# Attention scores: store tiles of 4 MB in runs of 32 KB, in place of 2 MB in runs of 16 KB

## Chip, cores, metric

One Trainium2 chip, one core. Its engines are PE (matrix products), ACT, DVE and POOL (elementwise work), and SP, which here issues the DMAs; 16 DMA engines carry the data. The metric is the device time of one execution in microseconds (us), the median of several runs. Spans in the profile are about 1.8 us shorter than that time.

## The reference

Inputs q and k of shape (8, 8, 512, 64): batch, heads, rows, dim. The output is `q @ k^T / 8` per head, (8, 8, 512, 512) in float32. 16.8 MB are read and 67.1 MB written.

```python
def reference(q, k):
    scale = 1.0 / np.sqrt(q.shape[-1])
    return (np.einsum('bhqd,bhkd->bhqk', q, k) * scale).astype(np.float32)
```

## The kernel before

The work goes in four units of two batches. Inputs are loaded, cast to bf16, transposed on PE, and copied into `kT` and into `qz`, a zero-padded block form with two heads in the 128 contraction rows. One matmul with 128 stationary columns then gives 64 rows of each of two heads. An output tile `o` holds 8 rows per partition (16 KB in one run), 2 MB in all, and four of them rotate. An eviction is the scaled copy of a finished product out of PE's accumulator memory into `o`.

```python
RO = 8                                   # output rows per partition
out_r = out.rearrange("(v b) (n h) (u i) k -> v (b n) (h u) (i k)", b=2, h=2, i=RO)
raw_pool = ...bufs=3    # xf, 16 KB per partition: one input tensor of one unit
out_pool = ...bufs=4    # o, 16 KB per partition
psum_pool = ...bufs=3   # ps, [128, 2, 512] f32, two banks
# ... cuts
def scores(v, n):
    kT, qz = ts[v]
    o = out_pool.tile([P, RO, S], f32, name="o")
    for i in range(0, RO, 2):
        ps = psum_pool.tile([P, 2, S], f32, name="ps")
        for w in range(2):
            nc.tensor.matmul(out=ps[:, w, :], lhsT=qz[:, i + w, n, :], rhs=kT[:, n]...)
        evacuate(o[:, i:i + 2, :], ps)    # x 1/8, alternately on ACT and DVE
        yield                             # steps of the next unit's transposes go in between
    nc.sync.dma_start(out=out_r[v, n], in_=src)
```

All loads and stores are issued from one queue (SP).

## Time and profile before

| | before |
|---|---|
| time, median (lowest to highest) | 204.17 us (204.15 to 204.36) |
| span in the profile, instructions in it | 202.3 us, 1549 |
| DVE, PE, ACT busy | 64%, 52%, 51% |
| loads and stores, share of 16 DMA engines' span | 97.7% |

The prediction below reads this profile. Two lines of the page's DMA section, not used there, become important later. They are the queues that fetch instructions. The columns are packets, MB, and share of the 16 engines' span.

```profile
q8 instruction: 4, 0.07, 0.1%
q14 instruction: 4, 0.03, 0.0%
```

In the trace's single DMA records, q8 carries packets of 16 KB and q14 packets of 8 KB.

### The profile page before, as it was taken

To read this page: it belongs to the slowest core of one execution; us is meant where nothing else is said; L and a number is where in the kernel's file an instruction comes from. 1 tells how busy PE (TensorE), PEld (TensorE's weight loads), DVE (VectorE), ACT (ScalarE), POOL (GpSimd) and SP (SyncE) were. 2 spreads that over 40 slices of the span, in tenths; PEclk is the share of its full clock that TensorE was granted. 3 is DMA by queue.
4 is the path that set the end of the run, shared out by engine and by line. 5 is a ranking of instruction groups with operands and counts; after the bars stand their busy time and mean duration, and the time that the engine had idled before them with its cause. 6 is when DMAs were issued, how large, how long until landed. Compare 5 with 4: busy or idle time off the path is not lost.

```text
span 202.3 us, 1549 instructions
## 1 busy us (share of the span) xinstructions
PE 106.1 (52%) x512; PEld 50.2 (25%) x512; DVE 129.6 (64%) x133; ACT 102.5 (51%) x130; POOL 26.8 (13%) x20
## 2 busy tenths in 40 slices
PE   0045557755854755858575575656564677642000
PEld 0034424432211322423222233223121222210000
DVE  6875669987765686878787788777544455553000
ACT  2254457967654448484756666574833344442000
POOL 1037775756000000000000000000000000000000
PEclk9999999978799699797979787896969655695555
DMA  6999999999999999999999999999999999999991
GB/s 214 428 441 428 424 441 421 424 395 434 437 421 434 432 423 431 434 428 428 437 424 431 431 424 434 434 428 431 434 428 428 431 434 428 428 437 429 416 447 75
DMA packets 5768, 83.99 MB, mean 415 GB/s; under 512 B 640, under 2 KB 640, under 8 KB 640
## 3 DMA queue, kind: packets, MB, share of 16 engines
q1 hardware_dynamic: 5760, 83.89, 97.7%
q8 instruction: 4, 0.07, 0.1%
q14 instruction: 4, 0.03, 0.0%
HBM read 16.78 MB, written 67.11 MB: 415 GB/s over the span
## 4 chain that ended last, share of the span: by engine, by line
DMA 52%; ACT 13%; DVE 13%; PE 10%; issue 2%; ACTq 0%; DVEq 0%; SPq 0%
DMA out_dram<-o 52%; ACT o L62 6%; DVE o L64 5%; PE ps L134 5%; ACT qz L99 4%; DVE qz L89 3%; ACT kT L99 3%; PE tp L120 3%; DVE kT L99 3%; PE tp L111 2%; DVE xb L83 1%; DVE qz L99 1%; ACTq L62 0%; DVEq L64 0%; SPq L140 0%
## 5 line engine op out<-in xcount | busy, mean ns | idle before, releaser
L134 PE MATMUL ps<-kT,qz 128*128 128x512 bf16 x256 | 87.3, 470 | 52.4 <-ACT o L62 43.3
L64 DVE TENSOR_SCALAR o<-ps 128x1024 f32<-128x1024 f32 x64 | 78.2, 1225 | 44.1 <-DMA out_dram<-o 28.5
L62 ACT ACTIVATE o<-ps 128x1024 f32<-128x1024 f32 x64 | 63.5, 1022 | 64.3 <-DMA out_dram<-o 50.9
L134 PEld LDWEIGHTS <-qz 128*128 128x128 bf16 x256 | 28.6, 115 | 98.6 <-issue 87.2
L83 POOL CAST xb<-xf 128x2048 bf16<-128x2048 f32 x14 | 26.1, 1893 | 21.5 <-DMA xf<-in_q_dram 18.1
L99 DVE COPY kT<-tp 64x512 bf16<-64x512 bf16 x32 | 22.0, 687 | 4.3 <-PE tp L111 3.8
L99 DVE COPY qz<-tp 64x512 bf16<-64x512 bf16 x32 | 22.0, 687 | 4.2 <-PE tp L120 3.7
L111 PE MATMUL tp<-identity,xb 128*128 128x128 bf16 x128 | 13.0, 267 | 17.0 <-DVE xb L83 11.1
L99 ACT COPY kT<-tp 64x512 bf16<-64x512 bf16 x32 | 18.5, 578 | 5.0 <-PE tp L111 4.7
L99 ACT COPY qz<-tp 64x512 bf16<-64x512 bf16 x32 | 18.5, 577 | 4.2 <-PE tp L120 3.9
L120 PE MATMUL tp<-identity,xb 128*128 128x128 bf16 x128 | 13.3, 271 | 8.1 <-ACT qz L99 4.9
L111 PEld LDWEIGHTS <-xb 128*128 128x128 bf16 x128 | 11.2, 122 | 21.3 <-ACT xb L83 11.1
L120 PEld LDWEIGHTS <-xb 128*128 128x128 bf16 x128 | 11.5, 123 | 12.6 <-issue 9.7
L89 DVE MEMSET qz<- 64x2048 uint32 x4 | 7.1, 1765 | 2.6 <-issue 1.4
L83 ACT CAST xb<-xf 128x2048 bf16<-128x2048 f32 x1 | 1.9, 1898 | 6.7 <-DMA xf<-in_k_dram 6.7
L83 ACT ACT_TABLE_LOAD x1 | 1.3, 1283 | 0.7 <-PEq L181 0.7
L83 DVE CAST xb<-xf 128x2048 bf16<-128x2048 f32 x1 | 1.2, 1227 | 0.0
masks.py:199 POOL TENSOR_SCALAR_AFFINE_SELECT identity<-identity 128x128 bf16<-128x128 bf16 x1 | 0.3, 292 | 0.1
masks.py:197 POOL MEMSET identity<- 128x128 bf16 x1 | 0.2, 205 | 0.3 <-POOLq L181 0.3
L181 POOL MEMSET const-float32-0.0<- 128x1 f32 x1 | 0.1, 98 | 0.2 <-issue 0.2
L181 POOL MEMSET const-bfloat16-1.0<- 128x1 bf16 x1 | 0.1, 101 | 0.0
L181 POOL MEMSET const-uint8-127<- 128x1 uint8 x1 | 0.1, 101 | 0.0
(1 smaller groups left out, 0.1 us busy)
## 6 DMA issues: line engine op xcount, KB each, us to landing
out_dram<-o SPq DMA_DIRECT2D x32, 2048.0 KB, 16.1
xf<-in_k_dram SPq DMA_DIRECT2D x4, 2048.0 KB, 11.3
xf<-in_q_dram SPq DMA_DIRECT2D x4, 2048.0 KB, 12.3
```

The source lines that it names most:

```text
L62: pinned(nc.scalar.mul(out=dst, in_=src, mul=scale))
L64: pinned(nc.vector.tensor_scalar(out=dst, in0=src, scalar1=scale, scalar2=None, op0=mybir.AluOpType.mult))
L83: pinned(copy(out=xb[:, :, s, :], in_=xf[:, s].rearrange("p (j d) -> p j d", j=J)))
L89: nc.vector.memset(qz[half(h), :, :, (1 - h) * U:(2 - h) * U], 0.0)
L99: pinned(copy(out=dst(s, h), in_=src[:, h]))
L111: pinned(nc.tensor.transpose(out=tp[:, j, :], identity=identity, in_=kb[:, j0 + j].rearrange("p s d -> p (s d)")))
L120: pinned(nc.tensor.transpose(out=tp[:, i, jj, :], identity=identity, in_=qb[:, RO * jj + i0 + i].rearrange("p s d -> p (s d)")))
L134: pinned(nc.tensor.matmul(out=ps[:, w, :], lhsT=qz[:, i + w, n, :], rhs=kT[:, n].rearrange("d m s j -> d (m s j)"), start=True, stop=True))
L181: nc = _bacc.Bacc("TRN2", target_bir_lowering=False, num_devices=1)
```

## The change

The intent: longer runs per store, so fewer DMA packets and fewer stores. A partition now holds 16 rows (32 KB in one run). A head then fills only 32 partitions, so a tile takes four heads: two head pairs, each in a 64-column tile of PE, side by side. 4 MB tiles need 32 KB per partition. Three such buffers are shared by inputs and outputs.

```diff
-    RO = 8
+    RO = 16
+    TILES = N // 2
-    out_r = out.rearrange("(v b) (n h) (u i) k -> v (b n) (h u) (i k)", b=2, h=2, i=RO)
+    out_r = out.rearrange("(v b) (t h) (u i) k -> v (b t) (h u) (i k)", b=2, h=4, i=RO)
-    raw_pool (bufs=3), out_pool (bufs=4), bf_pool (bufs=5)
+    big_pool (bufs=3), bf_pool (bufs=6)
-        if n_evac % 2 == 0:
+        if n_evac % 6 in (0, 2, 3):
 # load_and_cast: one buffer for k and q of a unit; all casts on GpSimd
-                if v == 0 and src is k_r:
-                    copy = (nc.vector.tensor_copy, nc.scalar.copy)[s]
 # scores
+        o = big_pool.tile([P, RO, S], f32, name="big")
             for w in range(2):
-                matmul(out=ps[:, w, :], lhsT=qz[:, i + w, n, :], rhs=kT[:, n]...)
+                for x in range(2):
+                    matmul(out=ps[half(x), w, :], lhsT=qz[:, i, 2 * t + x, :], rhs=kT[:, 2 * t + x]...)
-        nc.sync.dma_start(out=out_r[v, n], in_=src)
+        nc.sync.dma_start(out=out_r[v, t], in_=src)
```

(In the last matmul line `i` stands for `i + w`.) PE gets 512 matmuls and weight loads of 64 columns in place of 256 of 128, which is 512 more PE instructions.

More of the change, by code (lines that the diff above doesn't have):

```diff
@@ L42 @@
     k_r = k.rearrange("(v b) g (m j) d -> v (b g m) (j d)", b=2, j=R)
-    out_r = out.rearrange("(v b) (n h) (u i) k -> v (b n) (h u) (i k)", b=2, h=2, i=RO)
+    out_r = out.rearrange("(v b) (t h) (u i) k -> v (b t) (h u) (i k)", b=2, h=4, i=RO)
     consts = ctx.enter_context(tc.tile_pool(name="consts", bufs=1))
-    raw_pool = ctx.enter_context(tc.tile_pool(name="raw", bufs=3))
-    bf_pool = ctx.enter_context(tc.tile_pool(name="bf", bufs=5))
+    big_pool = ctx.enter_context(tc.tile_pool(name="big", bufs=3))
+    bf_pool = ctx.enter_context(tc.tile_pool(name="bf", bufs=6))
     t_pool = ctx.enter_context(tc.tile_pool(name="t", bufs=2))
-    out_pool = ctx.enter_context(tc.tile_pool(name="out", bufs=4))
     tpsum_pool = ctx.enter_context(tc.tile_pool(name="tpsum", bufs=2, space=bass.MemoryType.PSUM))
@@ L71, in load_and_cast @@
     def load_and_cast(v):
+        xf = big_pool.tile([P, 2, 2, J * D], f32, name="big")
         both = []
-        for src in (k_r, q_r):
-            xf = raw_pool.tile([P, 2, J * D], f32, name="xf")
-            nc.sync.dma_start(out=xf, in_=src[v])
+        for x, src in enumerate((k_r, q_r)):
+            nc.sync.dma_start(out=xf[:, x], in_=src[v].rearrange("p (s c) -> p s c", s=2))
+        for x in range(2):
             xb = bf_pool.tile([P, J, 2, D], bf16, name="xb")
             for s in range(2):
-                if v == 0 and src is k_r:
-                    copy = (nc.vector.tensor_copy, nc.scalar.copy)[s]
-                else:
-                    copy = nc.gpsimd.tensor_copy
-                pinned(copy(out=xb[:, :, s, :], in_=xf[:, s].rearrange("p (j d) -> p j d", j=J)))
+                pinned(nc.gpsimd.tensor_copy(out=xb[:, :, s, :],
+                                             in_=xf[:, x, s].rearrange("p (j d) -> p j d", j=J)))
             both.append(xb)
         return both
-    def clear(qz, h):
-        nc.vector.memset(qz[half(h), :, :, (1 - h) * U:(2 - h) * U], 0.0)
     def rearrange(tp, pattern, dst):
@@ L125, in transpose, with matmul, scores @@
                                  .rearrange("d i n (m s jj) -> d s i n m jj", s=2, jj=JJ)[:, s])
-    def scores(v, n):
+    def matmul(v, t, i, x, dst):
         kT, qz = ts[v]
-        o = out_pool.tile([P, RO, S], f32, name="o")
+        pinned(nc.tensor.matmul(out=dst, lhsT=qz[:, i, 2 * t + x, :],
+                                rhs=kT[:, 2 * t + x].rearrange("d m s j -> d (m s j)"),
+                                start=True, stop=True))
+    def scores(v, t):
+        o = big_pool.tile([P, RO, S], f32, name="big")
         for i in range(0, RO, 2):
@@ L133, in scores @@
             for w in range(2):
-                pinned(nc.tensor.matmul(out=ps[:, w, :], lhsT=qz[:, i + w, n, :],
-                                        rhs=kT[:, n].rearrange("d m s j -> d (m s j)"),
-                                        start=True, stop=True))
+                for x in range(2):
+                    matmul(v, t, i + w, x, ps[half(x), w, :])
             evacuate(o[:, i:i + 2, :], ps)
@@ L147 @@
     make_identity(nc, identity)
-    qzs = [consts.tile([P, RO, N, P], bf16, name=f"qz{n}") for n in range(2)]
+    qzs = [consts.tile([P, RO, N, 2 * U], bf16, name=f"qz{n}") for n in range(2)]
     for qz in qzs:
-        for h in range(2):
-            clear(qz, h)
+        nc.vector.memset(qz, 0.0)
     cast = [load_and_cast(v) for v in range(UNITS)]
@@ L158 @@
         ahead = transpose(v + 1, *cast[v + 1]) if v + 1 < UNITS else iter(())
-        per_step = 3 if v == 0 else 1
-        for n in range(N):
-            take(ahead, 1)
-            for _ in scores(v, n):
-                take(ahead, per_step)
+        for t in range(TILES):
+            for n, _ in enumerate(scores(v, t)):
+                take(ahead, 1 + (n % 4 == 3) if v else 2 * (t > 0))
         for _ in ahead:
```

## The prediction

> **What bounds the kernel now.** I read the page's busy shares and its DMA lines first, because 84 MB have to cross the DMA engines whatever the cores of the kernel do.
>
> ```profile
> span 202.3 us, 1549 instructions
> PE 106.1 (52%) x512; PEld 50.2 (25%) x512; DVE 129.6 (64%) x133; ACT 102.5 (51%) x130; POOL 26.8 (13%) x20
> ...
> DMA  6999999999999999999999999999999999999991
> ...
> q1 hardware_dynamic: 5760, 83.89, 97.7%
> ```
>
> No compute engine is over 64%. The DMA row is at nine tenths or more in every slice but the first and the last, and the one queue that carries all loads and stores fills 97.7% of 16 engines' span. The average could still hide a stage, so next the busy times by stretch.
>
> ```profile
> 0.00:5.00 5.00, 0.00 (x0) 0.00 (x0) 3.31 (x2) 1.28 (x1) 0.70 (x6) 1.00 0.68 216
> 5.00:30.00 25.00, 9.56 (x75) 8.01 (x76) 17.00 (x22) 11.34 (x18) 12.91 (x7) 1.00 1.00 430
> 30.00:50.00 20.00, 12.80 (x84) 7.32 (x83) 18.30 (x22) 15.92 (x23) 13.20 (x8) 0.90 1.01 421
> 50.00:100.00 50.00, 31.70 (x147) 13.84 (x146) 35.53 (x36) 28.93 (x35) 0.00 (x0) 0.87 1.01 430
> ...
> 195.00:202.30 7.30, 0.00 (x0) 0.00 (x0) 0.00 (x0) 0.00 (x0) 0.00 (x0) 0.50 0.44 189
> ```
>
> The columns after the window's length are PE, PE weight loads, DVE, ACT, POOL, then granted clock, DMA share and GB/s. DMA is full from 5 us to 195 us at 421 to 430 GB/s, also across the switch from loads to stores (30 to 50 us), the one place where compute is dense: DVE 18.3 of 20 us. Third, the waits.
>
> ```profile
> ACT o L62 <- DMA out_dram<-o: 50.9, 24, 3.0
> DVE o L64 <- DMA out_dram<-o: 28.5, 24, 2.0
> ```
>
> The evictions wait for a store to free their output buffer: compute is ahead of DMA by all four buffers. The chain of waits agrees: its largest part is the stores, 52%, in pieces of about 15 to 16 us, three or four queued stores long. So the end is set by: DMA starts at 1.7 us, each of 16 engines carries 320 packets of 16 KB plus 40 semaphore writes, and the tail. In the trace's single DMA records 4487 of the 5120 data packets took 611 ns and 635 of 640 semaphore writes 9 ns. That gives 320 x 0.611 + 40 x 0.009 = 195.9 us per engine; slow packets bring the mean to 197.6. The last data end at 201.0 us, though most engines are done by 198 to 199: a tail of some 2.5 us of unevenness.
>
> **What the Trainium skill says.** "DMA: Bandwidth & Descriptors", section "Where 436 GB/s comes from", puts the ceiling at 16 ports x 32 B x 850 MHz, 435.2 GB/s, or 27.2 GB/s per engine. 16 KB would then take 602.4 ns; the trace has 611, so at most 8.6 ns (1.4%) is not payload. The same page, section "Why small descriptors are slow (HBM only)", tells of a fixed cost of about 3 cycles per packet, 3.5 ns at that clock. The 9 ns of a 4-byte write is the size of the leftover too, which makes a fixed cost per packet plausible; no run so far separates it from a slightly lower rate per byte. On the matmuls, "TensorEngine Tiling (Array Packing)", section "Key Properties", says that tiles work in parallel, and its restrictions that column tiling turns off the fast weight load. "TensorE: Matmul & The Clock Gate", section "Measured speedup vs the span model", has 2.38x for three column tiles. The kernel before has no column tiles, so its trace can't agree or disagree.
>
> **The change part by part.**
>
> Stores. 32 stores of 2 MB become 16 of 4 MB; per engine 256 packets of 16 KB become 128 of 32 KB, if the packet follows the run. Loads keep their 64 packets of 16 KB. If the 8.6 ns are paid per packet, a 32 KB packet takes 2 x 602.4 + 8.6 = 1213.4 instead of 1222 ns: 128 x 0.0086 = 1.1 us less. Sixteen fewer DMAs save 16 x 0.009 = 0.14 us. Together 1.25 us, all on the path that sets the end, since DMA is never idle. This is all that the change can bring in the long run; even a perfect ceiling for all bytes (83.89 MB / 435.2 GB/s = 192.8 us against 197.6 busy) would be 4.8 us or 2.35%, and the loads aren't touched.
>
> Compute per 4 MB tile, off the path. It must fit under the 8 x 1.213 = 9.7 us of a store. One unit of four tiles (38.8 us) has 32 evictions: 16 on DVE and 16 on ACT, in a new pattern of three to three that changes no totals. DVE: 16 x 1.225 + 16 rearranging copies x 0.687 = 30.6 us. ACT: 16 x 1.022 + 16 x 0.578 = 25.6 us. Both fit, as now. PE: 128 matmuls of 64 columns in place of 64 of 128. From the warm stretches (four in 1.03 us, one alone 0.377) one starts each 0.218 us, so in parallel pairs 64 x 0.218 = 14 us and 5 us of transposes; strictly one after the other 28 + 5 = 33 us, still under 38.8, but with little room for waits.
>
> Buffers. Three of 4 MB in place of four of 2 MB. In the steady state a freed buffer has the two other stores, 19.4 us, less some 3 us of issue and landing, to be filled by 8 evictions and their copies, 8 to 10 us. Before it was 3 x 4.9 = 14.7 us less the same 3 for 4 to 5 us of work. Slack stays.
>
> The start, where the change could lose. Two things move. The first casts leave DVE and ACT: POOL does all, 1.87 us each and two per tensor. And the first store needs 8 evictions into a buffer that held the inputs of unit 1. The start of before, from the timeline:
>
> ```profile
> 8.68 1.90 ACT L83 CAST xb<-xf 128x2048 bf16<-128x2048 f32 x1 [6.66 <-DMA xf<-in_k_dram]
> ...
> 11.08 1.86 PE L111 MATMUL tp<-identity,xb 128*128 128x128 bf16 x16 [11.08 <-DVE xb L83]
> ...
> 13.58 3.73 POOL L83 CAST xb<-xf 128x2048 bf16<-128x2048 f32 x2 [12.28 <-DMA xf<-in_q_dram]
> ...
> 28.73 1.91 PE L134 MATMUL ps<-kT,qz 128*128 128x512 bf16 x4
> ...
> 34.34 39.41 SPq L140 DMA_DIRECT2D out_dram<-o  x9
> ```
>
> Key 0 lands at 8.7 in both; POOL is done with it at 8.7 + 3.7 = 12.4, so transposes begin 1.4 us later, and with the same 17 us of transposes and copies the first scores start near 29.3. Query 0 is cast by 13.6 + 3.7 = 17.3, before it is needed near 20.8. Inputs land every 4.9 us, so POOL keeps up: unit 1 is cast at 27 us (its buffer is free before 29.3), unit 2 at 37, unit 3 at 47. With the PE clock still low (a matmul each 0.43 us in before at 29 us) an eviction needs 0.86 us of parallel pairs: first eviction near 30.3, the eighth done near 30.3 + 7 x 0.9 + 1.2 = 37.8. The DMA queue has loads until about 1.7 + 64 x 0.611 + 0.9 (slow first packets) = 41.7. The first store is there 3 us early. The second tile, with two steps of the next transposes per eviction, takes some 9 us: 47, needed at 51. The third, in unit 3's buffer: 56, needed at 61. From there slack grows. No hole in the DMA row, then.
>
> Sum: 204.17 - 1.25 = 202.9 us.
>
> **The rivals.**
>
> *The 611 ns is a rate per byte.* Then 32 KB takes 1222 ns, and only the semaphores are saved: 204.0 us. For it: the 8.6 ns are inferred by a nominal clock. Against: the semaphore writes' 9 ns. I give it a third.
>
> *Column pairs run one after the other,* because a weight load for the other half waits, or without the fast load isn't hidden. Then an eviction costs 1.7 us at the low clock and 0.87 warm; the first tile is ready near 41 to 42 us, the DMA row gets a hole of about 1 us, and every tile with transposes takes 10 to 12 us against 9.7: 205 to 212 us. For it: alternate halves, twice the number of weight loads, PEclk falling to 5 or 6 tenths in places. Against: the skill's measured parallel column tiles;[...] compute has some 20 to 25% to spare.
>
> *Longer runs load the memory unevenly,* or engines drift apart more with packets twice as long. One step is 1.2 us in the tail, and the tail is already 2.5 us, set by one or two late engines: plus or minus 2 us, so 201 to 205. Nothing in before speaks of slower stores than loads: both take 611 ns.
>
> *A gain of over 2%* would need all bytes at the ceiling and a shorter tail as well. Nothing speaks for it.
>
> **Range and chances.** I take 203.1, between the first sum (202.9) and the rate-per-byte case (204.0), nearer the first. The range is 201.6 to 206.0: below by a shorter tail, above by a hole of 1 to 3 us at the start. Within 2% is 200.1 to 208.2. Faster 0.03, slower 0.07 (serial pairs that pace the tiles), within 0.90.
>
> **What would show it.** Store packets of 1213 ns (fixed cost) or 1222 (rate), or 16 KB packets in unchanged number (the run doesn't set the packet). The DMA row at nine all the way, above all at 40 to 45 us; first store issued before 41 us. Matmuls of the two halves starting a few ns apart, against 0.2 us or more. Evictions still waiting for stores, in sum near 80 us. The prediction is wrong if evictions wait chiefly for PE after 60 us, if a hole of over 3 us follows the loads, or if store packets take over 1240 ns.

## The result

The changed kernel takes 203.82 us (203.74 to 203.86, 4 runs) against 204.16 us before. The ratio is 0.9981, 95% interval 0.9964 to 0.9998. Ratios here are the mean time of one kernel's fast runs over that of the other's in the same rounds, so not quite the ratio of the quoted medians. The direction was right and the time lies in the range, but the gain is 0.34 us where 1.07 us were forecast.

The page of the changed kernel: span and instructions, busy time by engine, the DMA row by slice, and the DMA queues.

```profile
span 202.1 us, 1976 instructions
PE 107.7 (53%) x768; PEld 55.7 (28%) x768; DVE 126.4 (63%) x130; ACT 101.1 (50%) x129; POOL 30.5 (15%) x22
...
DMA  6999999999999999999999999999999999999991
...
q1 hardware_dynamic: 3456, 83.89, 97.2%
q8 instruction: 6, 0.10, 0.2%
q14 instruction: 2, 0.02, 0.0%
```

DMA is full as before, with no hole after the loads. The share of the data queue fell from 97.7 to 97.2% in almost the same span: there is more time in which some DMA engine is done. There are six large instruction fetches in place of four. The stretches of the changed kernel (window length; PE, PE weight loads, DVE, ACT, POOL; granted PE clock, DMA share, GB/s):

```profile
30.00:50.00 20.00, 12.12 (x108) 6.71 (x109) 14.37 (x17) 13.51 (x18) 13.10 (x8) 0.99 1.03 428
50.00:100.00 50.00, 35.06 (x278) 17.29 (x274) 42.96 (x47) 34.60 (x45) 0.00 (x0) 0.90 1.00 430
100.00:150.00 50.00, 35.11 (x227) 16.57 (x225) 35.81 (x37) 29.87 (x38) 0.00 (x0) 0.80 1.01 433
195.00:202.10 7.10, 0.00 (x0) 0.00 (x0) 0.00 (x0) 0.00 (x0) 0.00 (x0) 0.50 0.33 143
```

The middle runs at 430 to 433 GB/s against 430. The last stretch is emptier: DMA share 0.33 in 7.1 us, where it was 0.44 in 7.3 us. So most engines finish earlier, and the end does not come much earlier. The waits and the start, from the changed kernel's list of waits and then its timeline:

```profile
PE ps L126 <- ACT big L64: 36.6, 25, 4.7
DVE big L66 <- DMA out_dram<-big: 25.0, 9, 5.8
ACT big L64 <- DMA out_dram<-big: 24.5, 9, 4.9
ACT big L64 <- PE ps L126: 23.4, 25, 2.0
```

```profile
8.63 3.73 POOL L82 CAST xb<-big 128x2048 bf16<-128x2048 f32 x2 [7.33 <-DMA big<-in_k_dram]
...
12.41 1.89 PE L107 MATMUL tp<-identity,xb 128*128 128x128 bf16 x16 [12.41 <-POOL xb L82]
...
26.83 2.50 PE L126 MATMUL ps<-kT,qz 128*64 128x512 bf16 x12
...
35.05 9.35 SPq L141 DMA_DIRECT2D out_dram<-big  x2
```

Evictions still wait for stores, though 50 us in sum and not 79. Twelve 64-column matmuls took 2.50 us at the low clock: five steps of 0.43 us and one duration of 0.38 make 2.5, so two run in each step, their starts 3 to 4 ns apart, and the halves are parallel. (That 0.43 us belongs to the low clock is read from the trace's clock records: in both kernels matmuls, or pairs of them, start each 0.427 us where a record has 0.5 and each 0.215 us where it has 1.0. The first record, 1.0, begins at 28.9 us here and at 32.3 us before; the page draws the time ahead of it as full clock, but the pace there is 0.427.) The first store was issued at 35.1 us, before the loads' end near 42 us.

**Where the end comes from.** The page only has the mean of the 16 DMA engines. The trace also records each engine's semaphore write, which reports its part done, at the end of each load or store, so 16 times per DMA. These can be sorted into groups, as the engines differ by less than one store takes. In a group the earliest engine shows the pace without disturbance and the last one sets the end. For the last store (us from the span's start):

| | before | changed | difference |
|---|---|---|---|
| undisturbed engine per 4 MB stored | 9.724 | 9.681 | -0.043 |
| earliest engine done | 197.61 | 196.86 | -0.75 |
| last engine done | 201.00 | 200.75 | -0.25 |
| last minus earliest | 3.39 | 3.90 | +0.51 |

In every profile here the time is 3.0 to 3.2 us after the last engine's end. So the question has two parts: why the undisturbed engines gained 0.75 and not 1.25 us, and what made the last engine later by 0.51 us.

The records answer the first. A 32 KB packet is recorded with 1213 ns, exactly as forecast, against 2 x 611. But records of neighbouring packets overlap by about 4 ns: the next one starts 607 ns after the start of a 16 KB packet and 1209.5 after that of a 32 KB one. The gain is 4.7 ns for each packet that is no longer there, not 8.6.

For the second, two disturbances show. Around each 16 KB instruction fetch one engine's store packet takes 0.4 us more and the next starts 0.9 us late, 1.3 us in all. An 8 KB fetch costs 0.65 us. Each such engine stays late to the end. In the changed kernel the engines that a large fetch hit after the loads end 1.5 to 1.8 us after the earliest, so none of them is the last. And one engine drifts: its lateness against the median engine grows by 0.2 to 0.3 us per store from about 50 to 178 us, through packets that each take 10 to 100 ns more, and stops growing when the compute engines are done. It passes the others at about 110 us and sets the end, 3.90 us after the earliest. In the kernel before the same drift is there, 0.1 us per 2 MB store, and in its last 20 us that engine also jumps by 0.6 us, at the time of two 8 KB fetches.

A second engine has a part in this. In every profile one engine is already 1.8 to 2.9 us behind the earliest when the loads end, near 42 us, and but for run 2 it hardly moves after. In the kernel before it is the last one until about 170 us (2.75 us). It is a floor that less drift doesn't lower. The first large fetch falls just before, at 32 to 38 us, and may be a part of it; that was not tried.

### The profile page after: what moved, and what is told of

The parts are those of the page before. It is cut to its first block, busy times and chain, and to the rows that moved or that the text cites. A ratio compares the mean times of both kernels' runs of the same rounds, so it can differ in the third digit from the quotient of the medians.

```text
span 202.1 us, 1976 instructions
## 1 busy us (share of the span) xinstructions
PE 107.7 (53%) x768; PEld 55.7 (28%) x768; DVE 126.4 (63%) x130; ACT 101.1 (50%) x129; POOL 30.5 (15%) x22
## 3 DMA queue, kind: packets, MB, share of 16 engines
q1 hardware_dynamic: 3456, 83.89, 97.2%
## 4 chain that ended last, share of the span: by engine, by line
DMA 33%; DVE 14%; PE 6%; ACT 2%; issue 1%; DVEq 0%; ACTq 0%; SPq 0%
DMA out_dram<-big 33%; DVE big L66 9%; PE ps L126 6%; DVE kT L95 3%; ACT big L64 2%; DVE qz L95 1%; ACT kT L95 1%; PE tp L107 0%; DVEq L66 0%; ACTq L64 0%; SPq L141 0%
## 5 line engine op out<-in xcount | busy, mean ns | idle before, releaser
L126 PE MATMUL ps<-kT,qz 128*64 128x512 bf16 x512 | 85.0, 456 | 47.2 <-ACT big L64 36.6
L66 DVE TENSOR_SCALAR big<-ps 128x1024 f32<-128x1024 f32 x64 | 76.2, 1221 | 38.9 <-DMA out_dram<-big 25.0
L64 ACT ACTIVATE big<-ps 128x1024 f32<-128x1024 f32 x64 | 63.9, 1023 | 56.9 <-DMA out_dram<-big 24.5
L126 PEld LDWEIGHTS <-qz 128*64 128x64 bf16 x512 | 35.6, 124 | 85.9 <-issue 75.7
L82 POOL CAST xb<-big 128x2048 bf16<-128x2048 f32 x16 | 29.8, 1893 | 17.1 <-DMA big<-in_k_dram 9.6
L107 PE MATMUL tp<-identity,xb 128*128 128x128 bf16 x128 | 12.0, 253 | 15.0 <-POOL xb L82 12.4
L116 PE MATMUL tp<-identity,xb 128*128 128x128 bf16 x128 | 13.3, 272 | 7.8 <-ACT qz L95 4.1
L107 PEld LDWEIGHTS <-xb 128*128 128x128 bf16 x128 | 9.5, 114 | 20.8 <-POOL xb L82 12.4
L116 PEld LDWEIGHTS <-xb 128*128 128x128 bf16 x128 | 10.6, 123 | 14.4 <-issue 14.1
L151 DVE MEMSET qz<- 128x4096 uint32 x2 | 6.9, 3472 | 2.5 <-PEq L179 1.7
```

What stands on the lines that cost most here:

```text
L64: pinned(nc.scalar.mul(out=dst, in_=src, mul=scale))
L66: pinned(nc.vector.tensor_scalar(out=dst, in0=src, scalar1=scale, scalar2=None, op0=mybir.AluOpType.mult))
L82: pinned(nc.gpsimd.tensor_copy(out=xb[:, :, s, :], in_=xf[:, x, s].rearrange("p (j d) -> p j d", j=J)))
L107: pinned(nc.tensor.transpose(out=tp[:, j, :], identity=identity, in_=kb[:, j0 + j].rearrange("p s d -> p (s d)")))
L116: pinned(nc.tensor.transpose(out=tp[:, i, jj, :], identity=identity, in_=qb[:, RO * jj + i0 + i].rearrange("p s d -> p (s d)")))
L126: pinned(nc.tensor.matmul(out=dst, lhsT=qz[:, i, 2 * t + x, :], rhs=kT[:, 2 * t + x].rearrange("d m s j -> d (m s j)"), start=True, stop=T ...
```

## The experiments

The theory (A): the saving is 4.7 ns a packet; the end is set by one DMA engine that is slowed in proportion to the instructions executed, on top of instruction fetches that each delay one engine. Rivals: the full 8.6 ns are saved and lost elsewhere (B); run length is worth nothing (C); instructions off the critical path are free. All ratios are to the kernel before. "Earliest" and "last" are the engines of the table above, in the profiled run.

**1. Run length undone alone.** A pad cuts the buffer's row, and with it the run.

```diff
-        o = big_pool.tile([P, RO, S], f32, name="big")
+        o = big_pool.tile([P, A, RO * S // A + 16], f32, name="big")      # A = 2
-        nc.sync.dma_start(out=out_r[v, t], in_=src)
+        nc.sync.dma_start(out=out_r[v, t].rearrange("p (a c) -> p a c", a=A), in_=o[:, :, :RO * S // A])
```

> The changed kernel with each 4 MB store cut into runs of 16 KB (a pad in the buffer), all else the same: run length undone alone. Theory A (packets overlap by about 4 ns, so the saving was 43 ns per 4 MB store, and the end is set by one late DMA engine): store packets take 611 ns again, an undisturbed engine needs 9.72 us per 4 MB store against 9.68, and the time is 0.6 to 0.7 us over the changed kernel, near 204.4 us, so slightly over the kernel before. Theory B (the whole difference of the durations, 8.6 ns per packet, is saved): 9.75 us per store, 1.1 us more, 204.9 us. Rival C (run length is worth nothing, the small gain comes from the rest of the change): 203.8 us.

Measured: 204.08 us, ratio 0.9997 (0.9983 to 1.001). Packets took 611 ns and a store 9.719 us, as A said. The earliest engine ended 0.62 us later than in the changed kernel (197.48), but the last only 0.28 us later (201.03): the spread shrank from 3.90 to 3.55 us. So B and C fall, and A's figure for the time (0.6 to 0.7) is too high: run length is worth 0.6 us on an undisturbed engine and 0.26 us in time, by the medians.

**2. Runs of 4 KB**: the same edit with A = 8.

> The changed kernel with store runs of 4 KB: 64 store packets per engine and store in place of 8. The dose that measures the fixed cost of a packet. Theory A (some 4.6 ns a packet): 56 x 4.6 ns = 0.26 us per store, 16 stores 4.1 us, time near 207.9 us. Theory B (8.6 ns): 7.7 us, near 211.5 us.

Measured: 208.73 us, ratio 1.0223 (1.021 to 1.0237), between the two. In the first five stores an undisturbed engine needed 9.944 us per store, (9.944 - 9.681) / 56 = 4.7 ns a packet, as A said. From the sixth on most engines slowed, to about 10.2 us, some 9 ns a packet. Why is open. The spread of the engines here is only 1.79 us, and no engine drifts away.

**3. The column pairs undone alone** (wrong result: the second head pair gets the first one's keys). Stores stay as changed.

```diff
-                for x in range(2):
-                    matmul(v, t, i + w, x, ps[half(x), w, :])
+                matmul(out=ps[:, w, :], lhsT=qz[:, i + w, 2 * t:2 * t + 2, :]..., rhs=kT[:, 2 * t]...)
```

> Wrong on purpose: the changed kernel with one 128-column matmul in place of each pair of 64-column ones (the second head pair gets the keys of the first). 512 fewer PE instructions, stores and evictions the same. Theory A (the last DMA engine is late because something that grows with the number of instructions shares it, 2.9 us in before and 3.9 us in after, and instruction fetches take turns from DMA engines, 4 of 16 KB in before and 6 in after): its lateness falls by about 1 us, PE fetches fall to 4, time near 202.8 us, better than both kernels. Rival B (column pairs cost nothing off PE): 203.8 us.

Measured: 202.66 us, ratio 0.9929 (0.9916 to 0.9941). The page of this run:

```profile
span 200.9 us, 1455 instructions
...
q1 hardware_dynamic: 3456, 83.89, 97.6%
q8 instruction: 4, 0.07, 0.1%
q14 instruction: 2, 0.02, 0.0%
```

About 520 instructions and two large fetches fewer. The earliest engine ended at 196.87 us, as in the changed kernel; the last at 199.57, and the spread fell from 3.90 to 2.71 us. PE is no nearer to being the bound in either kernel, yet 1.16 us go, as the engine that drifts falls less far behind.

**4. A dose the other way**: ahead of every second matmul a tiny one (8 columns streamed) with its weight load; results unchanged.

```diff
+                    if x == 0:
+                        matmul(out=ps[half(x), w, :8], lhsT=qz[:, i + w, 2 * t, :], rhs=kT[:, 2 * t]...[:, :8])
                     matmul(v, t, i + w, x, ps[half(x), w, :])
```

> The changed kernel with 256 tiny extra matmuls (8 columns streamed) and their weight loads, 512 more PE instructions, results unchanged. Theory A: two more 16 KB instruction fetches (8), the late engine's lateness grows by about 1 us, time near 204.8 us. Rival B: PE has room, nothing changes, 203.8 us.

Measured: 204.81 us, ratio 1.0036 (1.0023 to 1.0048).

```profile
span 202.9 us, 2488 instructions
...
q8 instruction: 8, 0.13, 0.2%
```

Earliest 196.69, last 201.65, spread 4.96 us: 1.06 more for 512 instructions, about 2 ns each. Runs 3 and 4 together give (4.96 - 2.71) us / 1024 instructions = 2.2 ns. (The trace of run 3 lacks 9 matmuls.) No large fetch fell on the drifting engine in runs 3 and 4 or in the changed kernel: its lateness has no step of 1.3 us. And the extra time of slow packets after 42.5 us (8 to 200 ns over the usual 1213) goes with the number of instructions itself: 2.83 us in run 3, 3.95 in the changed kernel, 4.92 in run 4, so 2.6, 2.6 and 2.5 ns for each instruction started in that time.

**5. The dose on another engine**: 512 tiny memsets on POOL, which has nothing to do after its casts.

```diff
+    scratch = consts.tile([P, 8], f32, name="scratch")
+    for _ in range(512):
+        nc.gpsimd.memset(scratch, 0.0)
```

> The changed kernel with 512 tiny memsets on POOL after its casts, results unchanged. The 512 extra PE instructions of the run before cost 1.0 us, with the one slow DMA engine delayed about 2 ns more per instruction. Theory A1 (any engine's instruction costs that DMA engine about 2 ns): its lateness grows by about 1 us, now between 47 and 100 us, some fetches are added, time near 204.8 us. Rival A2 (only PE instructions, or what matmuls do, cost it): lateness as in the changed kernel, 203.8 us plus at most a little for the fetches.

Measured: 205.62 us, ratio 1.0076 (1.0063 to 1.0088).

```profile
span 204.1 us, 2488 instructions
...
q8 instruction: 6, 0.10, 0.2%
q14 instruction: 6, 0.05, 0.1%
```

No instruction uses what these memsets write. Still the last engine ended 2.1 us later (202.82; earliest 196.82; the profiled execution is the slowest of the five, 205.90 us). The slow packets sum to 6.6 us in place of 3.9, with nearly all of the surplus between 50 and 140 us, while POOL was busy with the memsets (48 to 131 us) or shortly after. The drifting engine's lateness has no step of a fetch here either. So it is not matmuls alone that go with the slowing: memsets on POOL do too, while ACT, DVE and SP were not dosed. A1 is right in kind; POOL's cost some 4 ns each by the last engine's end, 5 by the slow packets, and not 2.

**6. and 7. Less of the last store for the late engine.** Run 6 cut the last store into 112, 8 and 8 partitions; run 7 sent 28 KB of every partition in one store and the last 4 KB in 16 small ones.

```diff
 # run 6, last tile only
+            for a, b in ((0, 112), (112, 120), (120, 128)):
+                nc.sync.dma_start(out=out_r[v, t][a:b], in_=src[a:b])
 # run 7, last tile only
+            nc.sync.dma_start(out=out_r[v, t][:, :C], in_=src[:, :C])        # C = RO * S - 1024
+            for p in [32 * g + a for g in range(4) for a in range(4)]:
+                nc.sync.dma_start(out=out_r[v, t][p:p + 29:4, C:], in_=src[p:p + 29:4, C:])
```

> The changed kernel with its last 4 MB store cut in three by partitions: 112, 8 and 8. A store of 8 partitions should use only the eight lowest DMA engines, so these get 9 packets and the other eight 7 in place of 8 each. Theory A (one fixed DMA engine is late by 3.2 us and sets the end): if it is one of the upper eight it ends one packet, 1.2 us, earlier and the time falls to 202.7 to 203.2 us (the lower engines that an instruction fetch has hit then end last); if it is one of the lower eight the time rises to about 205.0 us. Rival (the lateness belongs to the queue's tail, not to an engine): 203.8 to 204.0 us.

> The unequal split again, without what spoiled the first try (packets of 2 to 4 us[...]). The last tile goes out as 28 KB of every partition, equal on all engines, and its last 4 KB as 16 small stores of 8 partitions four apart, which should use only the eight lowest engines. They get 8 packets of 4 KB more (about 1.2 us), the others 1.2 us less. Theory A with a late engine among the upper eight: last data near 199.6 to 200.1 us, time near 203.1 us, better than both kernels; among the lower eight: near 205 us. Rival (lateness of the tail, no fixed engine): 203.8 us. If the small stores go at under half speed, about 205 us too, and the packets' durations tell it from the second case.

Measured: 210.53 us, ratio 1.0322 (1.0308 to 1.0337), and 209.95 us, ratio 1.0282 (1.0268 to 1.0296). Both failed as remedies. In run 6, packets of the last store took up to 4 us in place of 1.2, so it tells nothing of the late engine. In run 7 packets were quick (1062 ns and 159 ns), but after the first seven small stores SP waited for stores to land (12.7 us in two waits) and then issued the rest one after the other, 0.67 us apart, each issue taking 0.63 us, until the last landed at 207 us. It did show one thing: the engine that finished its 28 KB part last, at 199.6 us, then carried small packets, seven in a row. It is thus one of the eight engines that an 8-partition store uses, and cannot be relieved in this way. The Trainium skill, page "DMA: Bandwidth & Descriptors", section "Why a DMA increments its semaphore by 16 and not by 1", says that such a store goes to the lowest-numbered engines. Eight engines for each small store is what run 7 shows; their numbers no run shows.

**8. Both undone**: the edits of runs 1 and 3 together, so that only the large buffers, the 16 stores and POOL's casts are left of the change. Its output is wrong, which doesn't matter for the time.

> Wrong on purpose: 128-column matmuls as in the third run and store runs of 16 KB as in the first, so that of the change only the large buffers, the 16 stores and the casts on POOL are left. Theory A (run length is worth 0.3 to 0.7 us also here, 512 PE instructions about 1.0 us): 202.9 to 203.4 us, so these other parts are worth 0.8 to 1.2 us against the kernel before. Rival (the two effects are not additive because short packets hide the slow engine): equal to the third run within 0.2 us, 202.5 to 202.8 us.

Measured: 203.07 us (four runs at 203.06 to 203.11, one at 203.78), ratio 0.9951 (0.9937 to 0.9965). That is A's figure, and shows that the parts which had looked like a mere means to the long runs are worth about 1.1 us by themselves. The profile is of the odd execution, 203.78 us. In it the drifting engine was already 0.86 us behind the earliest when the stores began, where the changed kernel has at most 0.3, so the same kernel's last engine can end 0.7 us later by chance. The slow packets sum to 2.5 us, fewer than in the changed kernel, as with run 3.

**9. A correct kernel of that kind**: the changed kernel with 8 rows per partition and 128-column matmuls again, two head pairs one behind the other in one 4 MB buffer and one store of two 16 KB runs per partition.

```diff
-    RO = 16
+    RO = 8
-        o = big_pool.tile([P, RO, S], f32, name="big")
+        o = big_pool.tile([P, 2, RO, S], f32, name="big")
+        for x in range(2):                       # n = 2 * t + x, the matmuls of the kernel before
-        nc.sync.dma_start(out=out_r[v, t], in_=src)
+        nc.sync.dma_start(out=out_r[v, 2 * t:2 * t + 2].rearrange("x p c -> p x c"), in_=o...)
```

> A correct kernel built from what the runs so far point to: the changed kernel's 4 MB buffers, 16 stores and casts, but the kernel before's 128-column matmuls (256 of them, 512 PE instructions fewer than the change) and its runs of 16 KB, two head pairs in one store. Theory A (late DMA engine slowed by instructions, 4 PE fetches, run length worth little): as the wrong-result run with 128 columns and 16 KB runs, 203.1 us, under both the kernel before and the changed one. Rival (the wrong-result run was fast because both halves read the same keys, or because its DMA went to one stretch of memory): 203.8 to 204.2 us.

> The changed kernel again, in the rounds of the run before, so that the two and the kernel before are compared on one chip. 203.8 us, ratio 0.998 to the kernel before; the profile should show the slow engine's lateness between 3.0 and 3.3 us again if it belongs to the kernel, and elsewhere if it is chance.

Measured, in the same rounds: run 9 is correct and takes 203.09 us, ratio 0.9949 (0.9936 to 0.9961). Run 10, the changed kernel again, takes 203.78 us, ratio 0.9982 (0.9968 to 0.9995), with a spread of 3.95 us: the lateness belongs to the kernel. The page of run 9:

```profile
span 201.2 us, 1464 instructions
...
q1 hardware_dynamic: 5504, 83.89, 98.1%
q8 instruction: 4, 0.07, 0.1%
q14 instruction: 2, 0.02, 0.0%
```

The earliest engine ended at 197.76 us, later than in the changed kernel and even than before, but the last at 199.95: the spread is 2.19 us. 98.1% is the highest share of all kernels here but run 2 (99.5%, with a spread of 1.79 us): the 16 engines end close together. The engine that was late when the loads ended ends 1.95 us after the earliest, so the drift sets only the last 0.25 us. In the last five stores even undisturbed engines slowed, from 9.719 to as much as 9.83 us, which is why the earliest ends late; it looks like run 2's slowing and is as open. This version beats both, with short runs.

| kernel | instructions | store run | 16 KB / 8 KB fetches | earliest | last | time |
|---|---|---|---|---|---|---|
| before | 1549 | 16 KB | 4 / 4 | 197.61 | 201.00 | 204.17 |
| changed | 1976 | 32 KB | 6 / 2 | 196.86 | 200.75 | 203.82 |
| 1 | 1976 | 16 KB | 6 / 2 | 197.48 | 201.03 | 204.08 |
| 3 (wrong result) | 1455 | 32 KB | 4 / 2 | 196.87 | 199.57 | 202.66 |
| 4 | 2488 | 32 KB | 8 / 2 | 196.69 | 201.65 | 204.81 |
| 5 | 2488 | 32 KB | 6 / 6 | 196.82 | 202.82 | 205.62 |
| 9 (correct) | 1464 | 16 KB | 4 / 2 | 197.76 | 199.95 | 203.09 |

## Why the prediction was right or wrong

**What bounds the kernel: right, but one level too coarse.** DMA is the bound before and after. But the text took the mean of 16 engines for the path. It saw the "tail of some 2.5 us of unevenness", even that one or two late engines set it, and put it into the range as plus or minus 2 us, where it is the path itself.

**The stores: the mechanism right, the term mis-sized.** The packets took the forecast 1213 ns. The failed term is "128 x 0.0086 = 1.1 us": records overlap by 4 ns, and start to start the fixed cost is 4.7 ns. 16 stores x 43 ns = 0.69 us, with the saved semaphores in it, is what an undisturbed engine gains, in place of the 1.25 us forecast; the earliest one gained 0.75 (three groups of stores before took 0.1 us more in sum).

**"All on the path that sets the end, since DMA is never idle": this step failed.** The last engine gained 0.25 us where the earliest gained 0.75. The change pays for its long runs with 512 PE instructions (runs 3 and 4: 1.2 and 1.0 us in time per 512). The two more large fetches came with them, but fell on engines that were not the last. It got that back from parts that the prediction had put at 0.14 us: 16 stores in place of 32 with the new buffers and casts, 1.1 us (run 8). Of these, the small fetches (2 in place of 4) are the visible candidate: before, the drifting engine stood 2.75 us behind the earliest and jumped by 0.63 us in the last 20 us, where two of them fall. The 85 fewer instructions would be another 0.2 us, an estimate from 2.2 ns each. Which of the parts earns how much was not tried.

That the time lay in the range and the sign came out right was luck: two effects of about 1 us each that the prediction did not have, +1.0 and -1.1, nearly cancelled.

**The sum by parts, from times:** large buffers, 16 stores, casts: -1.14 us (run 8 against before, same rounds). Column pairs at 16 KB runs: 204.08 - 203.07 = +1.01 us. Runs of 32 KB: 203.82 - 204.08 = -0.26 us. Together -0.39, against -0.34 measured; the runs come from different rounds, so a tenth is not to be read. With 128 columns the long runs were worth 202.66 - 203.07 = -0.41 us (run 3 against run 8).

**Compute, buffers and start: right.** No hole in the DMA row, evictions waiting for stores (50 us in sum, where near 80 were forecast), first store at 35.1 us. A weight load of 64 columns took 109 ns, where one of 128 columns had taken 98, and stayed hidden. The forecast for the first store was 38, because the next unit's transposes were put ahead of the first scores; the diff has none there.

**The rivals.** Serial column pairs: refuted by the 2.50 us of twelve matmuls. The rate per byte: refuted by 1213 ns and by run 1. The third, engines drifting apart, was the one that mattered, but it was tied to packet length. In run 2, with 4 KB packets, the spread is narrower, 1.79 us; in run 1, with 16 KB, it is 3.55 us and the drift goes on. What moves the drift in runs 3 to 5 is the count of instructions. Nothing in the page spoke for that; the DMA records did, had the last 4 us been read engine by engine before the prediction.

**What stays open.** What it is that slows one engine by 2 to 5 ns per instruction. It could be the recording of the trace; every run here lists a span and a clock, so an execution without recording is not among them. If it is, an unrecorded execution would not show the 1.0 us per 512 instructions. Why stores in 4 KB runs slow down after the fifth. What makes one engine late by the end of the loads.

## What to carry to other kernels

When DMA is full from start to end, the time is that of the latest DMA engine, not of the mean: look at how far apart the engines end before putting a saving per packet on the path. Then instructions cost time here even on engines with room to spare, 1 us per 512 on PE in 200 us, so a change that halves packets by doubling matmuls can cost more than it saves. Whether that holds when nothing is recorded, no run shows. Take a packet's cost from start to start, not from its recorded duration.

## What the Trainium skill lacked or had wrong

- "DMA: Bandwidth & Descriptors", section "Why small descriptors are slow (HBM only)": about 3 cycles of fixed cost per packet. That is 3.5 ns, an estimate, if the cycles are of the page's 850 MHz. Measured start to start: 4.7 ns, for 32 against 16 KB (run 1) and for 4 KB in the first five stores; later some 9 ns at 4 KB (run 2).
- "Runtime: NRT & Kernel Launch", section "Instruction fetch mechanics": says that instructions come in blocks of 16 KiB, 256 instructions, and that the fetch is mostly hidden. The size agrees for q8, which follows PE's instructions, and so does the count: about 1024 matmuls and weight loads, 4 fetches; 1536, 6; 2048, 8. It does not for q14: its fetches have 8 KB, four more for the 512 memsets on POOL (run 5), so 128 instructions each. What it lacks is that a fetch takes its turn on one of the 16 engines that carry the data and leaves that engine 1.3 us late (0.65 us for 8 KB), which a kernel bound by DMA doesn't make up.
- No page ties the lateness of a DMA engine to the number of executed instructions: about 2 ns per PE instruction (runs 3 and 4), 4 to 5 ns per POOL memset (run 5), in recorded executions.
- "TensorEngine Tiling (Array Packing)", section "Key Properties": tiles in parallel, which the trace shows (two 64-column matmuls per 0.43 us). It has no word on the doubled instructions as a cost outside PE: 1.0 us in 204 here.
